# Attention scores as 64-row products in the two halves of the array, with q's norm factor moved into the exponential

## The chip, the cores and the metric

The kernel runs on one core of a Trainium2 chip. The metric is the device time of one launch in microseconds (us), median of the runs shown. A core has a matrix engine (PE, with its weight loads as PEld), a vector engine (DVE), an activation engine (ACT), a general engine (POOL) and a queue engine that issues transfers (SP). Matrix products write to PSUM, which has eight banks here, shared out by the kernel under three tags: `mm` (3), `at` (4) and `tr` (1).

## The reference

One layer of a trunk: a norm, one projection to q, k, v and three convolution inputs, sliding-window attention beside a short gated convolution, an output projection, and a squared-ReLU MLP. S is 2048, D is 1024, 8 heads of 64, 2 key/value heads (each serves 4 heads), window and block 128. What the change touches is this:

```python
q = rms_norm(q, q_norm_g[l])          # over the 64 of each head
k = rms_norm(k, k_norm_g[l])
...
sc = jnp.einsum('bnqhgd,bnkhd->bnhgqk', qb, kw).astype(jnp.float32) * scale
...
sc = jnp.where(mask[None, :, None, None], sc, NEG_INF)
...
p = jax.nn.softmax(jnp.concatenate([sc, sink], axis=-1), axis=-1)[..., :-1]
o = jnp.einsum('bnhgqk,bnkhd->bnqhgd', p.astype(v.dtype), vw)
```

## The kernel before, in words

All large products are made of three: an operand is split into a high part (rounded to fp32r) and a low part (the rest), and high x high, high x low and low x high are summed in PSUM (`mm3`, lines 276 to 280).

The 2048 rows go through the mixers in four chunks of 512 (`mixers`, line 1031), each of four blocks of 128 rows; `b` counts blocks from 0 to 15. The MLP follows: its up products are line 1454, its down products line 1571. In the mixers, two streams of work are woven together. One is attention block by block: `qk_norm` (line 675), `qk_transpose` (689), `softmax` (712), `values` (752). The other is `besides` (978), a generator of the large products: the convolution's inputs (`pc`, `px`, `pb`), the output projection (`pout`), and q, k, v of the next chunk (`pz`). The table `FILL` says how many steps of the second are taken between the pieces of the first, the table `PRIO` shifts the priority of the first, and a scheduler then sets each engine's order when the program is built. So a block's score products stand on PE either in one run, or one by one between large products.

For one block of 128 rows, before the change:

- `qk_norm` squares the 640 columns of q and k (line 679), sums by head (681), takes the power -1/2 on POOL (192, 193), multiplies all of q and k by that factor `rq` (684) and by the norm weights (687).
- `qk_transpose` turns q (four 128x128 transposes, line 697) and k (699) on PE. q's turned columns hold two heads each, one in partitions 0 to 63 and one in 64 to 127. Each head gets an operand `qt` of 128 rows, its high part in one half of the partitions and its low part in the other (702, 703). k gets, for each key/value head, two such operands `kw`, with the parts so placed that both products of a head are a full 128 rows deep (704 to 707).
- `softmax` makes two products per head, of 128 rows and 256 columns (128 keys of the block before and 128 of this one; 128 columns in block 0): 16 products a block at line 724, two heads to a bank of tag `at`. ACT copies this block's half out of the bank (732), and DVE writes the earlier block's scores over the keys that lie ahead of the query, one head at a time (735). Maximum (737, 738), eight exponentials with their sums (741), the sink (745, 746) and the division (749) follow.

The first products of a block after the scores are the transposes of its probabilities (line 760). The norm weights are loaded in `load_gains` (496, 497) and q's is scaled by 1/8 on POOL (1104). Chunk 0 has its own start (`first_chunk`, line 518), with hand-ordered engines; it writes q into `z` at line 622. Later chunks write it at line 663.

Of the kernel before, what the change touches and what calls it, by code (L numbers as in the profile page):

```python
# [16 lines left out]
P = 128  # L17
# [87 lines left out]
def hymba_layer(  # L105
# [60 lines left out]


# [320 lines left out]
    g_qk = const.tile([P, 2, DH], F32, name="g_qk")  # L488
# [5 lines left out]
    def load_gains(part):  # L494
        if not part:
            nc.sync.dma_start(g_qk[:, 0, :], q_norm_g[0].partition_broadcast(P))
            nc.sync.dma_start(g_qk[:, 1, :], k_norm_g[0].partition_broadcast(P))
            nc.sync.dma_start(sink, sinks[0].partition_broadcast(P))
            return
        for t in range(3):  # L500
            nc.sync.dma_start(cw[:, :, t], conv_w[0][t].rearrange("(i p) -> p i", p=P))
        nc.sync.dma_start(g_cols, mlp_norm_g[0].rearrange("(k p) -> p k", p=P))
        for kv in range(KVH):
            nc.sync.dma_start(
                g_y[kv * DH : (kv + 1) * DH, 0, :],
                attn_out_g[0][kv * GQ * DH : (kv + 1) * GQ * DH].rearrange("(i d) -> d i", d=DH),
            )
        nc.sync.dma_start(g_y[:, 1, :], conv_out_g[0].rearrange("(i p) -> p i", p=P))
# [9 lines left out]
    def first_chunk(first):  # L518
# [102 lines left out]
        for t in range(NT):  # L621
            nc.scalar.activation(z0[t][:, :AW], pzs[t], AF.Copy, scale=rs0[:, t : t + 1])
# [14 lines left out]
    with tc.tile_pool(name="mix_small", bufs=1) as mix_small, tc.tile_pool(name="mix", bufs=1) as mix:  # L637
# [3 lines left out]
        kw = mix.tile([P, 2, KVH, 2, P], F32R, name="kw")  # L641
# [6 lines left out]
        def project_qkv(c, h, z):  # L648
# [5 lines left out]
            for pc, t in ((0, 0), (0, 1), (1, 0), (0, 2), (0, 3), (1, 1), (1, 2), (1, 3)):  # L654
# [8 lines left out]
                nc.scalar.copy(z[t][:, pc * AW : pc * AW + n], ps)  # L663
                if pc and not t:
                    qk_norm(c * NT, z[0])
# [6 lines left out]
        nh = HEADS + KVH  # L672
        mix_small.tile([P, 8], F32, name="mix_pad")

        def qk_norm(b, zt):
# [8 lines left out]
            nc.vector.tensor_tensor(zqk, zqk, rq[:, :, None].to_broadcast([P, nh, DH]), op=ALU.mult)  # L684
            for i, (h0, h1) in enumerate(((0, HEADS), (HEADS, nh))):
                nc.vector.tensor_tensor(
                    zqk[:, h0:h1], zqk[:, h0:h1], g_qk[:, i, None, :].to_broadcast([P, h1 - h0, DH]), op=ALU.mult
                )
        def qk_transpose(b, zt):
# [3 lines left out]
            lo, hi = slice(0, DH), slice(DH, P)  # L693
            qt = mix.tile([P, HEADS // 2, 2, P], F32R, tag="qt", name=f"qt_{nm}", bufs=1)
            pt = bank("at", f"ptq_{nm}")
            for j in range(4):
                nc.tensor.transpose(pt[:, j * P : (j + 1) * P], zt[:, j * P : (j + 1) * P], ident)
            pk = bank("at", f"ptk_{nm}")[:, :P]
            nc.tensor.transpose(pk, zt[:, O_K:O_V], ident)
            p3 = pt.rearrange("p (j q) -> p j q", j=4)  # L700
            for i, (a, o) in enumerate(((lo, hi), (hi, lo))):
                nc.scalar.copy(qt[a, :, i, :], p3[a])
                nc.vector.tensor_tensor(qt[o, :, i, :], p3[a], qt[a, :, i, :].bitcast(F32), op=ALU.subtract)
                nc.scalar.copy(kw[a, i, i, own, :], pk[a])
                nc.scalar.copy(kw[o, 1 - i, i, own, :], pk[a])
                nc.vector.tensor_tensor(kw[o, i, i, own, :], pk[a], kw[a, i, i, own, :].bitcast(F32), op=ALU.subtract)
# [5 lines left out]
        def softmax(b, qt):  # L712
# [6 lines left out]
            for pr in range(HEADS // 2):  # L719
                kv = pr * 2 // GQ  # L720
                ps = bank("at", f"psc_{nm}_{pr}").rearrange("p (h s k) -> p h s k", h=2, s=2)
                for j in range(2):
                    for r in range(2):
                        nc.tensor.matmul(  # L724
                            ps[:, j].rearrange("p s k -> p (s k)")[:, :nk],
                            qt[:, pr, j, :],
                            kw[:, r, kv, :, :].rearrange("p s k -> p (s k)")[:, :nk],
                            start=r == 0,
                            stop=r == 1,
                        )  # L730
                s2 = sc[:, pr * 2 : pr * 2 + 2, :]
                nc.scalar.copy(s2, ps[:, :, own, :])  # L732
                for j in range(2):
                    other = ps[:, j, 1 - own, :] if b else neg.to_broadcast([P, P])
                    nc.vector.copy_predicated(s2[:, j, :], later, other)  # L735
            ngm = mix_small.tile([P, HEADS], F32, tag="ngm", name=f"ngm_{nm}", bufs=2)
            nc.vector.tensor_reduce(ngm, sc, axis=AX.X, op=ALU.max, negate=True)
            nc.vector.tensor_tensor(ngm, ngm, nsink, op=ALU.min)  # L738
            den = mix_small.tile([P, HEADS], F32, tag="den", name=f"den_{nm}", bufs=2)
            for hd in range(HEADS):  # L740
                nc.scalar.activation(  # L741
                    sc[:, hd, :], sc[:, hd, :], AF.Exp, bias=ngm[:, hd : hd + 1], accum_out=den[:, hd : hd + 1]
                )
# [287 lines left out]
        def mixers(c, before, h, z):  # L1031
# [20 lines left out]
            def scores(t):  # L1052
# [3 lines left out]
                with ahead(1):  # L1056
                    sc = softmax(c * NT + t, qt)
                if t + 1 < NT:
                    with ahead(2):
                        qk_norm(c * NT + t + 1, z[t + 1])  # L1060
                return sc

            if not c:
                qk_norm(0, z[0])
# [38 lines left out]
        with tc.issue_after(rs0_in):  # L1103
            nc.gpsimd.tensor_scalar(g_qk[:, 0, :], g_qk[:, 0, :], DH**-0.5, None, op0=ALU.mult)
# [506 lines left out]
```

## Time and profile before

| what | value |
|---|---|
| time, median of 3 runs | 1917.67 us (1916.55 to 1918.78) |
| profiled execution: its span, first to last instruction | 1913.4 us |
| median less that span | 4.3 us |
| PE busy | 1907.7 us, 8930 products |
| PEld busy | 1591.1 us |
| DVE busy | 1202.7 us, 1857 instructions |
| ACT busy | 829.4 us, 1557 instructions |
| POOL busy | 274.4 us, 477 instructions |
| granted PE clock | 1.000 |

No time of the profiled execution is given beside its span; the 4.3 us between the span and the median of the runs is taken as what lies around a span. A product's recorded duration is longer than the distance to the next one, since products overlap on PE; what a product costs is read from the distances between starts. In a row of the timeline the columns are start, duration of the stretch, engine, line, operation, output and inputs, rows x columns of the weights, shape of the operand, and how many were merged.

### The profile page before, as it was taken

The numbers are of one execution on the slowest core, as the hardware profiler recorded it, in microseconds if no ns is written. First come the engines' busy times: TensorE is split into PE (matmuls) and PEld (weight loads), VectorE is DVE, ScalarE is ACT, GpSimd is POOL, SyncE is SP. The second block draws the span as 40 slices with busy tenths as digits, with TensorE's granted clock in tenths as the row PEclk, the third lists the DMA queues.
The fourth block names the chain that finished last, engine by engine and source line by source line (L and its number), as shares of the span: only waits on it lengthen the run. The fifth ranks groups of instructions, "written<-read, shape, count | busy, mean of one in ns | idle before, by whom it ended". The sixth has DMA issues, their size and how long they took to land.

```text
span 1913.4 us, 24557 instructions
## 1 busy us (share of the span) xinstructions
PE 1907.7 (100%) x8930; PEld 1591.1 (83%) x8930; DVE 1202.7 (63%) x1857; ACT 829.4 (43%) x1557; POOL 274.4 (14%) x477
## 2 busy tenths in 40 slices
PE   9999999999999999999999999999999999999999
PEld 8888888888888888888888888888888888888887
DVE  5895567448467759998788766666534334457531
ACT  6564245335445346544555545453332332232320
POOL 2123212302221112233101111111000000100000
PEclk9999999999999999999999999999999999999999
DMA  9984844564578688777576544448954457766631
GB/s 305 333 320 120 329 189 177 213 227 160 203 266 277 215 294 251 221 215 244 195 233 213 175 145 159 140 148 321 364 198 150 138 171 224 281 228 213 217 124 55
DMA packets 232792, 413.80 MB, mean 216 GB/s; under 512 B 51672, under 2 KB 136416, under 8 KB 219872
## 3 DMA queue, kind: packets, MB, share of 16 engines
q1 hardware_dynamic: 203840, 336.59, 52.0%
q0 software_dynamic: 15424, 51.40, 6.9%
q10 hardware_dynamic: 13408, 24.26, 3.4%
q8 instruction: 70, 1.15, 0.2%
q14 instruction: 50, 0.41, 0.1%
HBM read 286.35 MB, written 125.83 MB: 215 GB/s over the span
## 4 chain that ended last, share of the span: by engine, by line
PE 99%; DVE 0%; POOL 0%; issue 0%; ACT 0%; DVEq 0%; POOLq 0%
PE u L1454 32%; PE d L1571 32%; PE pout L278 3%; PE pout L280 3%; PE pout L279 3%; PE pz L278 2%; PE pz L280 2%; PE pz L279 2%; PE psc_b L724 2%; PE pb_c L280 2%; PE pb_c L279 2%; PE pb_c L278 2%; PE px_c L278 2%; PE px_c L279 2%; PE px_c L280 2%; PE po_b L812 1%
## 5 line engine op out<-in xcount | busy, mean ns | idle before, releaser
L1454 PE MATMUL u<-op_x,wop 128*128 128x512 f32 x2688 | 609.7, 389 | 0.0
L1571 PE MATMUL d<-op_w,op_f 128*128 128x512 f32 x2691 | 609.5, 389 | 0.0
L1571 PEld LDWEIGHTS d<-op_w,op_f 128*128 128x128 f32 x2691 | 504.8, 188 | 104.7
L1454 PEld LDWEIGHTS u<-op_x,wop 128*128 128x128 f32 x2688 | 504.3, 188 | 105.3 <-issue 0.3
L434 DVE TENSOR_TENSOR op_f<-op_f 128x1024 fp32r<-128x1024 f32 x112 | 136.8, 1224 | 235.6 <-ACT op_f L433 235.4
L433 ACT CAST op_f<-op_f 128x1024 fp32r<-128x1024 f32 x112 | 117.7, 1051 | 349.5 <-DMA op_f<-fop 349.0
L452 ACT CAST wop<-wu 128x512 fp32r<-128x512 f32 x156 | 96.1, 619 | 92.0 <-PE u L1454 88.3
L453 DVE TENSOR_TENSOR wop<-wu,wop 128x512 fp32r<-128x512 f32 x156 | 110.2, 708 | 31.8 <-ACT wop L452 16.7
L1190 POOL DMA_DIRECT2D fop<-s x96 | 52.1, 542 | 443.2 <-DVE s L1193 436.7
L1196 DVE TENSOR_TENSOR u<-u,u 128x512 f32<-128x512 f32 x128 | 87.7, 685 | 19.4 <-PE u L1454 19.2
L434 DVE TENSOR_TENSOR op_w<-raw,op_w 128x1024 fp32r<-128x1024 f32 x56 | 68.3, 1221 | 28.8 <-ACT op_w L433 28.8
L433 ACT CAST op_w<-raw 128x1024 fp32r<-128x1024 f32 x56 | 58.8, 1052 | 48.4 <-PE d L1571 26.3
L1202 ACT ACTIVATE u<-u 128x512 f32<-128x512 f32 x64 | 40.5, 632 | 56.5 <-DVE u L1196 54.3
L741 ACT ACTIVATE sc_b<-sc_b,ngm_b 128x128 f32<-128x128 f32 x128 | 49.7, 389 | 30.0 <-DVE ngm_b L738 30.0
L773 POOL TENSOR_SCALAR_AFFINE_SELECT pp_b<-pp_b 128x512 fp32r<-128x512 f32 x60 | 41.3, 701 | 134.6 <-ACT pp_b L766 66.1
L1403 POOL DMA_DIRECT2D wds<-raw x16 | 8.5, 533 | 329.9 <-DVE raw L1401 329.9
L453 DVE TENSOR_TENSOR wop<-wu_s,wop 128x512 fp32r<-128x512 f32 x64 | 45.9, 718 | 11.9 <-ACT wop L452 11.7
L452 ACT CAST wop<-wu_s 128x512 fp32r<-128x512 f32 x64 | 39.4, 620 | 29.3 <-PE u L1454 24.9
L278 PE MATMUL pout<-w_wo,yt_c 128*128 128x512 f32 x128 | 51.5, 402 | 0.0
L280 PE MATMUL pout<-w_wo,yt_c 128*128 128x512 f32 x128 | 51.0, 398 | 0.0
L279 PE MATMUL pout<-w_wo,yt_c 128*128 128x512 f32 x128 | 50.2, 393 | 0.0
L735 DVE COPY_PREDICATED sc_b<-later,psc_b 128x128 f32<-128x128 int32 x120 | 29.4, 296 | 32.0 <-ACT sc_b L732 31.7
(265 smaller groups left out, 3119.0 us busy)
## 6 DMA issues: line engine op xcount, KB each, us to landing
op_f<-fop SPq DMA_DIRECT2D x112, 512.0 KB, 4.3
raw<-in_w_down_dram SPq DMA_DIRECT2D x72, 512.0 KB, 4.1
wu<-in_w_up_dram SPq DMA_DIRECT2D x128, 256.0 KB, 3.8
w_wo<-wo SPq DMA_DIRECT2D x24, 1024.0 KB, 6.7
fop<-s POOLq DMA_DIRECT2D x96, 256.0 KB, 2.6
fop<-u ACTq DMA_DIRECT2D x64, 256.0 KB, 2.6
op_x<-xop SPq DMA_DIRECT2D x28, 512.0 KB, 6.0
w_q<-q SPq DMA_DIRECT2D x12, 1024.0 KB, 6.7
```

The source lines that it names most:

```text
L278: nc.tensor.matmul(ps, st(0), mv(0), start=first, stop=False)
L279: nc.tensor.matmul(ps, st(0), mv(1), start=False, stop=False)
L280: last_sum[0] = nc.tensor.matmul(ps, st(1), mv(0), start=False, stop=last).ins
L433: nc.scalar.copy(op[:, 0], raw)
L434: nc.vector.tensor_tensor(op[:, 1], raw, op[:, 0].bitcast(F32), op=ALU.subtract)
L452: splits.append(nc.scalar.copy(hi, blk).ins)
L453: lows.append(nc.vector.tensor_tensor(lo, blk, hi.bitcast(F32), op=ALU.subtract).ins)
L741: nc.scalar.activation(sc[:, hd, :], sc[:, hd, :], AF.Exp, bias=ngm[:, hd : hd + 1], accum_out=den[:, hd : hd + 1])
L1190: eng.dma_start(fop_dram[tb][ORDER_DOWN.index(i)][n // 2][:, n % 2], b)
L1196: return nc.vector.tensor_tensor(dst, ps, b, op=ALU.add).ins
L1454: nc.tensor.matmul(pt, wops[i][:, a, k, :], xops[tb, p][k // 2][:, b, k % 2, :], start=p not in GOES_ON and k + j == 0, stop=k + j == NB + ...
L1571: nc.tensor.matmul(ps[tb][j][:, cs], fs[tb][:, a, k, j * P : (j + 1) * P], w[:, b, k, cs], start=first and p not in GOES_ON and k + n == 0 ...
```

## The change

- Heads are stored so that a group of 128 columns of q holds one head of each key/value head (`by_pair`, used where q is written to `z`). After the transpose, partitions 0 to 63 hold a head that uses key head 0, and 64 to 127 a head that uses key head 1.
- `qt` and `kw` hold the high and the low part of both halves in the same partitions. A score is the sum of three products of 64 rows (high x high, high x low, low x high), with the two key heads' products issued in turn, into two different banks: 24 products a block.
- q is not multiplied by its norm factor any more. The factor is applied to the negated maximum and given to the exponential as its scale, head by head. k is still multiplied by its factor.
- The two norm weights and 1/8 are multiplied into one column `g_qk`, applied to turned k as it is copied out of PSUM.
- The masked write takes two heads in one instruction.

```diff
-            nc.sync.dma_start(g_qk[:, 0, :], q_norm_g[0].partition_broadcast(P))
-            nc.sync.dma_start(g_qk[:, 1, :], k_norm_g[0].partition_broadcast(P))
+            for kv in range(KVH):
+                for i, g in enumerate((q_norm_g, k_norm_g)):
+                    nc.sync.dma_start(g_qk2[kv * DH : (kv + 1) * DH, i : i + 1], g[0].rearrange("(d i) -> d i", i=1))
...
-            nc.scalar.activation(z0[t][:, :AW], pzs[t], AF.Copy, scale=rs0[:, t : t + 1])
+            nc.scalar.activation(by_pair(z0[t]), by_kv(pzs[t]), AF.Copy, scale=rs0[:, t : t + 1])
...
-                nc.scalar.copy(z[t][:, pc * AW : pc * AW + n], ps)
+                if pc:
+                    nc.scalar.copy(z[t][:, AW:], ps)
+                else:
+                    nc.scalar.copy(by_pair(z[t]), by_kv(ps))
...
-            nc.vector.tensor_tensor(zqk, zqk, rq[:, :, None].to_broadcast([P, nh, DH]), op=ALU.mult)
-            for i, (h0, h1) in enumerate(((0, HEADS), (HEADS, nh))):
-                nc.vector.tensor_tensor(
-                    zqk[:, h0:h1], zqk[:, h0:h1], g_qk[:, i, None, :].to_broadcast([P, h1 - h0, DH]), op=ALU.mult
-                )
+            zk = zqk[:, HEADS:]
+            nc.vector.tensor_tensor(zk, zk, rq[:, HEADS:, None].to_broadcast([P, KVH, DH]), op=ALU.mult)
+            return rq
...
-            for i, (a, o) in enumerate(((lo, hi), (hi, lo))):
-                nc.scalar.copy(qt[a, :, i, :], p3[a])
-                nc.vector.tensor_tensor(qt[o, :, i, :], p3[a], qt[a, :, i, :].bitcast(F32), op=ALU.subtract)
-                nc.scalar.copy(kw[a, i, i, own, :], pk[a])
-                nc.scalar.copy(kw[o, 1 - i, i, own, :], pk[a])
-                nc.vector.tensor_tensor(kw[o, i, i, own, :], pk[a], kw[a, i, i, own, :].bitcast(F32), op=ALU.subtract)
-                nc.vector.tensor_tensor(
-                    kw[a, 1 - i, i, own, :], pk[a], kw[a, i, i, own, :].bitcast(F32), op=ALU.subtract
-                )
+            nc.scalar.copy(qt[:, 0], p3)
+            nc.vector.tensor_tensor(qt[:, 1], p3, qt[:, 0].bitcast(F32), op=ALU.subtract)
+            nc.scalar.activation(kw[:, 0, own, :], pk, AF.Copy, scale=g_qk)
+            nc.vector.scalar_tensor_tensor(
+                kw[:, 1, own, :], pk, g_qk, kw[:, 0, own, :].bitcast(F32), op0=ALU.mult, op1=ALU.subtract
+            )
...
-            for pr in range(HEADS // 2):
-                kv = pr * 2 // GQ
-                ps = bank("at", f"psc_{nm}_{pr}").rearrange("p (h s k) -> p h s k", h=2, s=2)
+            for g0 in range(0, GQ, 2):
+                pss = [bank("at", f"psc_{nm}_{g0}_{kv}").rearrange("p (h s k) -> p h s k", h=2, s=2) for kv in range(KVH)]
                 for j in range(2):
-                    for r in range(2):
-                        nc.tensor.matmul(
-                            ps[:, j].rearrange("p s k -> p (s k)")[:, :nk],
-                            qt[:, pr, j, :],
-                            kw[:, r, kv, :, :].rearrange("p s k -> p (s k)")[:, :nk],
-                            start=r == 0,
-                            stop=r == 1,
-                        )
+                    for n, (a, r) in enumerate(((0, 0), (0, 1), (1, 0))):
+                        for kv in range(KVH):
+                            rows = slice(kv * DH, (kv + 1) * DH)
+                            nc.tensor.matmul(
+                                pss[kv][:, j].rearrange("p s k -> p (s k)")[:, :nk],
+                                qt[rows, a, g0 + j, :],
+                                kw[rows, r].rearrange("p s k -> p (s k)")[:, :nk],
+                                start=n == 0,
+                                stop=n == 2,
+                            )
...
-                for j in range(2):
-                    other = ps[:, j, 1 - own, :] if b else neg.to_broadcast([P, P])
-                    nc.vector.copy_predicated(s2[:, j, :], later, other)
+                    other = ps[:, :, 1 - own, :] if b else neg[:, :, None].to_broadcast([P, 2, P])
+                    nc.vector.copy_predicated(s2, later[:, None, :].to_broadcast([P, 2, P]), other)
...
+            nc.vector.tensor_tensor(by_kv1(ngm), by_kv1(ngm), by_pair1(rq), op=ALU.mult)
...
-                    sc[:, hd, :], sc[:, hd, :], AF.Exp, bias=ngm[:, hd : hd + 1], accum_out=den[:, hd : hd + 1]
+                    sc[:, hd, :],
+                    sc[:, hd, :],
+                    AF.Exp,
+                    bias=ngm[:, hd : hd + 1],
+                    scale=rq[:, i : i + 1],
+                    accum_out=den[:, hd : hd + 1],
...
-            nc.gpsimd.tensor_scalar(g_qk[:, 0, :], g_qk[:, 0, :], DH**-0.5, None, op0=ALU.mult)
+            nc.gpsimd.tensor_tensor(g_qk, g_qk2[:, :1], g_qk2[:, 1:], op=ALU.mult)
+        with tc.issue_after(rs0_in):
+            nc.gpsimd.tensor_scalar(g_qk, g_qk, DH**-0.5, None, op0=ALU.mult)
```

Two places on PE's order show how the score products stand. The first is block 1 (in chunk 0), where they stand in one run between products of the convolution (`pb_c0`, 128x512). In the names, `psc_b1_0` is a bank of block 1's scores, `kw` and `qt_b1` its operands; 128x256 is the output. Before:

```order
L280 MATMUL pb_c0_0_1_973<-h0_a0_250,w_wb0_1_905 128x512
L724 MATMUL psc_b1_0_996<-kw_631,qt_b1_942 128x256 x4
L724 MATMUL psc_b1_1_1004<-kw_631,qt_b1_942 128x256 x4
L724 MATMUL psc_b1_2_1012<-kw_631,qt_b1_942 128x256 x4
L724 MATMUL psc_b1_3_1020<-kw_631,qt_b1_942 128x256 x4
L278 MATMUL pb_c0_0_1_973<-h0_a0_250,w_wb0_0_904 128x512
```

The same place on PE after the change, its first nine rows (`psc_b1_0_0` is the bank of key head 0 and `psc_b1_0_1` that of key head 1; 16 more rows of the same kind follow before the next product of the convolution):

```order
L296 MATMUL pb_c0_0_1_962<-h0_a0_250,w_wb0_1_902 128x512
L742 MATMUL psc_b1_0_0_985<-kw_634,qt_b1_939 128x256
L742 MATMUL psc_b1_0_1_986<-kw_634,qt_b1_939 128x256
L742 MATMUL psc_b1_0_0_985<-kw_634,qt_b1_939 128x256
L742 MATMUL psc_b1_0_1_986<-kw_634,qt_b1_939 128x256
L742 MATMUL psc_b1_0_0_985<-kw_634,qt_b1_939 128x256
L742 MATMUL psc_b1_0_1_986<-kw_634,qt_b1_939 128x256
L742 MATMUL psc_b1_0_0_985<-kw_634,qt_b1_939 128x256
L742 MATMUL psc_b1_0_1_986<-kw_634,qt_b1_939 128x256
```

Sixteen full products have become 24 half ones that alternate between the halves of the array, still in one run. The second place is block 4 (in chunk 1) on PE, where the scores stand between the convolution's products (`px_c1`). Before:

```order
L724 MATMUL psc_b4_0_2358<-kw_631,qt_b4_2289 128x256
L280 MATMUL px_c1_0_0_2469<-h0_h1_1425,w_wx01_1_2466 128x512
L724 MATMUL psc_b4_0_2358<-kw_631,qt_b4_2289 128x256
L278 MATMUL px_c1_0_0_2469<-h0_h1_1425,w_wx01_0_2465 128x512
L724 MATMUL psc_b4_0_2358<-kw_631,qt_b4_2289 128x256
L279 MATMUL px_c1_0_0_2469<-h1_h1_1426,w_wx01_0_2465 128x512
L724 MATMUL psc_b4_0_2358<-kw_631,qt_b4_2289 128x256
L280 MATMUL px_c1_0_0_2469<-h0_h1_1425,w_wx01_1_2466 128x512
```

After, in block 4, on PE:

```order
L742 MATMUL psc_b4_2_0_2350<-kw_634,qt_b4_2271 128x256
L295 MATMUL px_c1_0_1_2490<-h1_h1_1413,w_wx01_0_2442 128x512
L742 MATMUL psc_b4_2_1_2351<-kw_634,qt_b4_2271 128x256
L296 MATMUL px_c1_0_1_2490<-h0_h1_1412,w_wx01_1_2443 128x512
L742 MATMUL psc_b4_2_0_2350<-kw_634,qt_b4_2271 128x256
L294 MATMUL px_c1_0_1_2490<-h0_h1_1412,w_wx01_0_2442 128x512
L742 MATMUL psc_b4_2_1_2351<-kw_634,qt_b4_2271 128x256
L295 MATMUL px_c1_0_1_2490<-h1_h1_1413,w_wx01_0_2442 128x512
```

Here too three half products stand where two full ones stood, and a full 512-column product still stands between one half product and the next. Counted over the whole program, 256 score products in 113 runs become 384 in 157 runs; 140 of these runs are one to three products long and hold 161, and 17 runs of four to 24 hold the other 223.

More of the change, by code (lines that the diff above doesn't have):

```diff
@@ L165, in zrow, with by_kv, by_kv1, by_pair1 @@
         return pool.tile([P, O_B], F32, tag="z", name=name, bufs=NT)
+    def by_kv(b):
+        return b.rearrange("p (v g d) -> p v g d", v=KVH, g=GQ)
+    def by_kv1(r):
+        return r.rearrange("p (v g) -> p v g", v=KVH)
+    def by_pair1(r):
+        return r[:, :HEADS].rearrange("p (g v) -> p v g", v=KVH)
+    def by_pair(zt):
+        return zt[:, :AW].rearrange("p (g v d) -> p v g d", v=KVH, g=GQ)
     ident = const.tile([P, P], F32, name="ident")
@@ L672, in hymba_layer @@
         nh = HEADS + KVH
+        rqs = {}
         mix_small.tile([P, 8], F32, name="mix_pad")
```

31 lines of the change are left out of this document (17 added, 14 removed).

## The prediction

> **What bounds the kernel now.** I read the page first, for who is busy, and its chain of waits, for who sets the end:
>
> ```profile
> span 1913.4 us, 24557 instructions
> PE 1907.7 (100%) x8930; PEld 1591.1 (83%) x8930; DVE 1202.7 (63%) x1857; ACT 829.4 (43%) x1557; POOL 274.4 (14%) x477
> PE 99%; DVE 0%; POOL 0%; issue 0%; ACT 0%; DVEq 0%; POOLq 0%
> ```
>
> PE has work in all of the span, and the chain is PE itself for 99% of it. DVE and ACT are busy for 63% and 43%. The view of waits, limited to PE, has a single row:
>
> ```profile
> PE idle L579 <- POOL ident L172: 1.6, 1, 1.6
> ```
>
> That one is at the very start. So an edit changes the time by what it changes in PE's own products, and by waits that it would newly make. Next, what a product costs. The groups by line, and the timeline of PE around block 1's scores (in one run) and block 4's (one by one):
>
> ```profile
> L1454 PE MATMUL u<-op_x,wop 128*128 128x512 f32 x2688 | 609.7, 389 | 0.0
> ...
> L724 PE MATMUL psc_b<-kw,qt_b 128*128 128x256 f32 x240 | 47.1, 284 | 0.0
> ```
>
> ```profile
> 78.63 2.08 PE L724 MATMUL psc_b<-kw,qt_b 128*128 128x256 f32 x16
> ...
> 80.55 0.40 PE L278 MATMUL pb_c<-h_a,w_wb 128*128 128x512 f32 x1
> ```
>
> ```profile
> 226.13 0.28 PE L724 MATMUL psc_b<-kw,qt_b 128*128 128x256 f32 x1
> 226.25 0.40 PE L280 MATMUL px_c<-h_h,w_wx 128*128 128x512 f32 x1
> 226.48 0.28 PE L724 MATMUL psc_b<-kw,qt_b 128*128 128x256 f32 x1
> ```
>
> A 512-column product stands 609.7 / 2688 = 0.227 us after the one before, though its record lasts 0.389: the records overlap, and distances are the cost. A score product in a run costs (80.55 - 78.63) / 16 = 0.120. One that stands alone costs 226.48 - 226.13 - 0.227 = 0.123. Block 0's have 128 columns:
>
> ```profile
> 59.93 1.90 PE L724 MATMUL psc_b<-kw,qt_b 128*128 128x128 f32 x16
> 61.67 0.45 PE L278 MATMUL px_c<-h_a,w_wx 128*128 128x512 f32 x1
> ```
>
> They cost (61.67 - 59.93) / 16 = 0.109. From 512 to 256 columns the cost falls by 0.107, so half of that again would leave 0.120 - 0.053 = 0.067 for 128. It is 0.109: something that doesn't shrink with the columns takes at least that long for each product, and the weight load, one per product, is the candidate. All scores now: 16 x 0.109 + 240 x 0.121 = 30.8 us.
>
> **The change part by part.** *Score products.* 256 full products become 384 half ones, with as many columns as before. A half product has half the rows, and nothing in the three spacings above depends on rows, so alone it should cost what a full one does. The gain can only come from two halves that run together. The order after the change has 223 half products in 17 runs of four or more and 161 in 140 short runs, mostly alone between 512-column products that use all rows; those find no partner. The trace before has no product in half the rows, so what a pair costs is bounded from both sides:
>
> - Nothing runs together: each half product costs what a full one does, 24 x 0.109 + 360 x 0.120 = 45.8, so +15.0.
> - Streams overlap but loads follow one another: in runs the load sets the pace. That is 24 x 0.109 for block 0, 199 x 0.109 for the other products in runs and 161 x 0.122 for those in short runs, together 2.6 + 21.7 + 19.6 = 43.9, so +13.1.
> - A pair costs what one full product does: block 0 has 12 x 0.109, the other runs of four or more have 101 pair places (a run of odd length leaves one alone) x 0.120, the short runs 142 x 0.122; 1.3 + 12.1 + 17.3 = 30.7, so -0.1. Even in this best case the runs only give back what the lone products lose.
>
> I take the middle of the first two, +14, since both follow from the row nearest to the case (0.109 a product at half the columns), and pairing rests on nothing that this trace shows.
>
> *Change of shape.* Each of the 157 runs means two changes between full products and half ones, 314 in all. The trace has one product with few rows, `pg`, whose weights have 8:
>
> ```profile
> 2.59 1.49 PE L579 MATMUL idle<-ident 128*128 128x128 f32 x6
> 4.01 0.27 PE L583 MATMUL pg<-ident,g_rows 8*128 8x8 f32 x1
> 4.21 1.11 PE L540 MATMUL pt_a<-ident,x 128*128 128x128 f32 x4
> 5.12 1.06 PE L579 MATMUL idle<-ident 128*128 128x128 f32 x4
> ```
>
> Products here stand about 0.214 apart, so the last of the six starts at 3.66. `pg` follows 0.35 later and `pt_a` 0.20 after that: 0.55 for two distances that would be 0.43. Two changes cost at most 0.12 here, 0.06 each, and a wait for the loaded rows may be in it; the low end is nothing. The far end is that PE empties first: a 512-column record outlasts the distance by 0.389 - 0.227 = 0.162. So 314 changes cost 0 to 19 us by `pg`, and 51 by a full emptying. The forecast takes nothing, and the emptying is a rival.
>
> *DVE and ACT.* The groups that change:
>
> ```profile
> L703 DVE TENSOR_TENSOR qt_b<-ptq_b,qt_b 64x512 fp32r<-64x512 f32 x32 | 22.0, 689 | 7.8 <-ACT qt_b L702 7.1
> L684 DVE TENSOR_TENSOR z<-z,rq_b 128x640 f32<-128x640 f32 x16 | 14.5, 908 | 26.1 <-POOL rq_b L193 26.1
> L706 DVE TENSOR_TENSOR kw<-ptk_b,kw 64x128 fp32r<-64x128 f32 x32 | 9.0, 282 | 0.6 <-ACT kw L705 0.3
> L735 DVE COPY_PREDICATED sc_b<-later,psc_b 128x128 f32<-128x128 int32 x120 | 29.4, 296 | 32.0 <-ACT sc_b L732 31.7
> L738 DVE TENSOR_TENSOR ngm_b<-ngm_b,nsink 128x8 f32<-128x8 f32 x16 | 2.6, 160 | 0.2
> L702 ACT CAST qt_b<-ptq_b 64x512 fp32r<-64x512 f32 x32 | 18.6, 580 | 17.6 <-PE ptq_b L697 9.2 <-DVE qt_b L703 7.0 <-PE psc_b L724 1.1
> L705 ACT CAST kw<-ptk_b 64x128 fp32r<-64x128 f32 x32 | 8.3, 260 | 0.4
> L741 ACT ACTIVATE sc_b<-sc_b,ngm_b 128x128 f32<-128x128 f32 x128 | 49.7, 389 | 30.0 <-DVE ngm_b L738 30.0
> ```
>
> One of two 0.69 us subtractions goes, all but a fifth of line 684's 0.91 (est. 0.7), about the same again for the norm weights of line 687 over the same columns, three of four 0.28 subtractions for `kw` (0.84), and some 0.1 of each pair of masked writes (est. 0.4 a block); 0.16 comes in for the scaled maximum: 3.2 us a block, 51 for 16 blocks, off DVE. ACT loses one of two 0.58 casts and three of four 0.26 casts, 1.4 a block, 22 in all; if the scale from memory adds 0.1 to each of 128 exponentials, 13 of it come back. No row has PE waiting for either engine, so I cost all this at nothing. If that cover were gone (the fill products between scores and probabilities), a later exponential would delay line 760's transposes; with ACT and DVE both shorter there is less of that than before, and I allow 2 us either way.
>
> *Waits that move.* A pair of banks is now let go after 12 products (1.4 us at 0.120) instead of one bank after four, so ACT's first copy starts about 1 us later. Behind it in ACT's queue stand casts of weights, and products of `besides` cover both. The exponential now also waits for `rq`, but q's transposes no longer do, so that factor has more time than before. SP issues four small loads in place of two, ahead of `sink`, and POOL one product of one column more; neither has a wait of PE behind it in the view above, and both stand in the first microseconds behind x and the weights. Nothing for them.
>
> *Sum.* 1913.4 + 14 = 1927.4 of span. The median of the runs shown is 4.3 above this span, so 1931.7, say 1932.
>
> **The rivals.** *A: pairs run together, changes of shape are free.* Then -0.1 from above, within 2 or 3: about 1918. For it: the two halves' products alternate and write different banks. By the Trainium skill, TensorE: Matmul & The Clock Gate, Part 3, products in different row groups run at once (four of 32 rows gave 3.07 times the rate). No run here shows it yet, and by that rule the sum would be this rival's. Against it: 0.109 for each load, if two loads don't run together.
>
> *B: a change of shape makes PE empty.* With pairs together and 314 changes at 0.06 to 0.162, +19 to +51: 1937 to 1969, the middle 1953; without pairs up to +66, 1984. It decides from about 0.05 a change, where it outweighs what pairing could bring. The Trainium skill, TensorEngine Tiling (Array Packing), Key Properties, says that changing the tiling mode drains the engine, without a time; by that rule this rival holds, and `pg`, at 0.06 or less a change, speaks for its low end.
>
> *C: faster.* A lone half product leaves the other half free, and the next full product, or its load, gets ahead there. If a lone half cost 0.061 instead of 0.122, the 142 places would save 8.7: with pairs, 1909. It decides when the distance from one lone score product to the next falls below 0.32, from 0.35 now. Against it: full products need all rows, and block 0's 0.109 is not bound by columns.
>
> **How the numbers follow.** The forecast has 0.39, A 0.22, B 0.29, C 0.10. About 0.2%, 4 us, is what a measurement of this kernel can tell from no change. A with its 3 us is nearly all "same" (0.20, the rest slower), C is faster, and the forecast and B are slower: 0.10, 0.20 and 0.70. The range begins under A with a part of C, 1913, and ends at B's 1969; outside are most of C and B without pairs, together under 0.2. The forecast's own range is 1929 to 1936.
>
> **What would show it.** In block 1's run, the distance from the first half product to the next convolution product, over 24: 0.109 to 0.120 bears the forecast out, 0.060 means pairs (A). In chunk 1, from one lone half product to the next across a 512-column one: 0.35 is no price for shape, 0.47 or more is B, under 0.32 is C. PE's waits should stay near 1.6 us, and DVE lose some 50 us. A wait of PE for ACT or DVE in the mixers, or a gain of over 5 us, would make the working wrong.

## The result and the profile after

| what | before | after |
|---|---|---|
| median of 4 runs | 1918.22 us (1916.55 to 1920.19) | 2044.03 us (2039.95 to 2045.91) |
| ratio, 95% interval | | 1.0655 (1.064 to 1.067) |
| profiled execution: span | 1913.4 us | 2044.2 us |
| stage of the mixers (start to first up product) | 690.5 us | 804.5 us |
| stage of the up products | 609.6 us | 623.1 us |
| stage of the down products | 613.3 us | 616.6 us |

The change costs 126 us, far above the range. The prediction had the sign, and neither the size nor the parts. The page of the kernel after, first the span, the busy times, the granted clock of PE in 40 slices, and the chain of waits by engine:

```profile
span 2044.2 us, 24584 instructions
...
PE 2031.5 (99%) x9058; PEld 1623.2 (79%) x9058; DVE 1156.2 (57%) x1713; ACT 821.6 (40%) x1493; POOL 276.8 (14%) x478
...
PEclk9999878999997899999999999999999999999999
...
PE 82%; DMA 0%; issue 0%; POOL 0%; DVE 0%; ACT 0%; DVEq 0%; ACTq 0%
```

PE is still the bound and still shows 99% busy, but its record is 124 us longer for 128 more products. DVE lost 46.5 us, ACT 7.8. What is new is the clock: 7s and 8s stand in two places where before there were only 9s. Next the stages after, by windows (columns: length, then busy time and count for PE, PEld, DVE, ACT and POOL, granted clock, share of the DMA engines, GB/s):

```profile
0.00:804.50 804.50, 795.62 (x3680) 615.32 (x3681) 398.01 (x747) 315.90 (x777) 148.75 (x266) 0.93 0.57 203
804.50:1427.60 623.10, 623.10 (x2690) 503.17 (x2689) 479.73 (x696) 331.51 (x543) 105.38 (x168) 1.00 0.63 199
1427.60:2044.20 616.60, 612.77 (x2692) 504.66 (x2690) 278.46 (x270) 174.16 (x174) 22.72 (x44) 1.00 0.60 205
```

The same three before the change:

```profile
0.00:690.50 690.50, 688.64 (x3551) 582.17 (x3552) 445.41 (x891) 323.79 (x841) 147.95 (x265) 1.00 0.65 237
690.50:1300.10 609.60, 609.60 (x2690) 504.33 (x2689) 478.99 (x696) 330.89 (x543) 103.75 (x168) 1.00 0.62 203
1300.10:1913.40 613.30, 609.43 (x2692) 504.57 (x2690) 278.31 (x270) 174.75 (x174) 22.72 (x44) 1.00 0.60 206
```

114.0 us of the 130.8 lie in the mixers, where the scores are. The other 16.8 lie in the MLP, whose code the change doesn't touch and whose clock is 1.00. Groups of the kernel after that answer to the prediction's:

```profile
L1482 PE MATMUL u<-op_x,wop 128*128 128x512 f32 x2688 | 623.3, 393 | 0.0
...
L742 PEld LDWEIGHTS psc_b<-kw,qt_b 64*128 64x128 f32 x384 | 47.3, 207 | 49.7 <-issue 48.8
L742 PE MATMUL psc_b<-kw,qt_b 64*128 64x256 f32 (+1 forms) x384 | 84.8, 371 | 0.0
...
L762 ACT ACTIVATE sc_b<-sc_b,ngm_b,rq_b 128x128 f32<-128x128 f32 x128 | 61.5, 482 | 27.5 <-DVE ngm_b L758 27.5
```

An up product now stands 623.3 / 2688 = 0.232 us from the next, 0.227 before. The weight loads of the scores have a wait of 48.8 us ahead of them that the trace can lay on nothing but the issue. The scale from memory costs an exponential 482 - 389 = 93 ns. Now the two places that the prediction named, on PE's timeline. Block 1's run:

```profile
81.14 0.39 PE L296 MATMUL pb_c<-h_a,w_wb 128*128 128x512 f32 x1
81.45 1.69 PE L742 MATMUL psc_b<-kw,qt_b 64*128 64x256 f32 x24
83.07 0.50 PE L294 MATMUL pb_c<-h_a,w_wb 128*128 128x512 f32 x1
83.41 0.40 PE L295 MATMUL pb_c<-h_a,w_wb 128*128 128x512 f32 x1
```

The 24 half products take 83.07 - 81.45 = 1.62, or 0.068 each. Twelve pairs at 0.12 make 1.44, so halves do run together, and 0.18 is left over at the run's end. The distance into the run is 0.31 where two such products stand 0.227 apart, and the product behind it stands 0.34 ahead of its follower. The three excesses, 0.08, 0.18 and 0.11, make 0.37 for the run. Chunk 1, lone halves, first at full clock and then a little later:

```profile
232.79 0.38 PE L742 MATMUL psc_b<-kw,qt_b 64*128 64x256 f32 x1
233.10 0.49 PE L296 MATMUL px_c<-h_h,w_wx 128*128 128x512 f32 x1
233.53 0.38 PE L742 MATMUL psc_b<-kw,qt_b 64*128 64x256 f32 x1
...
239.73 0.58 PE L742 MATMUL psc_b<-kw,qt_b 64*128 64x256 f32 x1
...
240.96 0.58 PE L742 MATMUL psc_b<-kw,qt_b 64*128 64x256 f32 x1
```

From one lone half to the next it is 0.74 (0.35 before), later 1.23. In between, the granted clock has fallen, which a window shows:

```profile
237.10:261.00 23.90, 23.90 (x47) 12.76 (x47) 6.21 (x11) 2.13 (x6) 0.19 (x1) 0.50 0.33 136
```

Nine such stretches at 0.50 lie in the mixers, 112.6 us together (the clock record of the trace: 3.4, 23.9, 20.5, 10.2 and 6.8 us in chunks 0 and 1, 3.4, 20.5, 17.1 and 6.8 in chunk 3). Before there was none. In the 3.4 us ahead of eight of the nine, PE's record has no gap and holds four to eight score products among larger ones; ahead of the first, at 63.1 us, PE has waited 1.5 us for ACT. Last, PE's waits, the first three of eight rows that make 8.7 us:

```profile
PE pt_a L322 <- DVE h_h L327: 2.4, 4, 0.8
PE idle L597 <- POOL ident L188: 1.6, 1, 1.6
PE ptq_b L717 <- ACT sc_b L752: 1.5, 1, 1.5
```

All but the second are new, 7.1 us in sum. The prediction had no wait of PE for DVE or ACT.

**The theory** after this reading: each run of half products costs about 0.39 us beside the work in it, whatever its length (0.74 - 0.35); lone halves between full products also bring PE's clock down; buffers that have moved cost the MLP its 17 us; and the order that the other edits bring costs a few us of waits. **The rivals:** the loss is one of 24 products instead of 16; the other edits make it; the price is one per half product; the clock falls by half products as such.

### The profile page after: what moved, and what is told of

Same layout as the page of the kernel before. It is cut to its first block, busy times and chain, and to the rows that moved or that the text cites. A ratio compares the mean times of both kernels' runs of the same rounds, so it can differ in the third digit from the quotient of the medians.

```text
span 2044.2 us, 24584 instructions
## 1 busy us (share of the span) xinstructions
PE 2031.5 (99%) x9058; PEld 1623.2 (79%) x9058; DVE 1156.2 (57%) x1713; ACT 821.6 (40%) x1493; POOL 276.8 (14%) x478
## 4 chain that ended last, share of the span: by engine, by line
PE 82%; DMA 0%; issue 0%; POOL 0%; DVE 0%; ACT 0%; DVEq 0%; ACTq 0%
PE u L1482 30%; PE d L1599 30%; PE pout L294 2%; PE pout L296 2%; PE pout L295 2%; PE psc_b L742 2%; PE pz L294 1%; PE pz L295 1%; PE pz L296 1%; PE po_b L838 1%; PE pc_c L294 1%; PE pb_c L296 1%; PE pc_c L295 1%; PE pb_c L295 1%; PE pc_c L296 1%; PE pb_c L294 1%
## 5 line engine op out<-in xcount | busy, mean ns | idle before, releaser
L1482 PE MATMUL u<-op_x,wop 128*128 128x512 f32 x2688 | 623.3, 393 | 0.0
L742 PEld LDWEIGHTS psc_b<-kw,qt_b 64*128 64x128 f32 x384 | 47.3, 207 | 49.7 <-issue 48.8
L742 PE MATMUL psc_b<-kw,qt_b 64*128 64x256 f32 (+1 forms) x384 | 84.8, 371 | 0.0
L449 ACT CAST op_w<-raw 128x1024 fp32r<-128x1024 f32 x56 | 58.6, 1048 | 45.1 <-PE d L1599 20.5
L762 ACT ACTIVATE sc_b<-sc_b,ngm_b,rq_b 128x128 f32<-128x128 f32 x128 | 61.5, 482 | 27.5 <-DVE ngm_b L758 27.5
L752 ACT COPY sc_b<-psc_b 128x256 f32<-128x256 f32 x64 | 21.8, 374 | 119.8 <-PE psc_b L742 119.7
L754 DVE COPY_PREDICATED sc_b<-later,psc_b 128x256 f32<-128x256 int32 x60 | 24.4, 440 | 66.2 <-ACT sc_b L752 66.1
L294 PE MATMUL pout<-w_wo,yt_c 128*128 128x512 f32 x128 | 52.0, 406 | 0.3 <-DVE x L989 0.3
```

Source lines behind the costliest of these rows:

```text
L294: nc.tensor.matmul(ps, st(0), mv(0), start=first, stop=False)
L449: nc.scalar.copy(op[:, 0], raw)
L742: nc.tensor.matmul(pss[kv][:, j].rearrange("p s k -> p (s k)")[:, :nk], qt[rows, a, g0 + j, :], kw[rows, r].rearrange("p s k -> p (s k)")[ ...
L762: nc.scalar.activation(sc[:, hd, :], sc[:, hd, :], AF.Exp, bias=ngm[:, hd : hd + 1], scale=rq[:, i : i + 1], accum_out=den[:, hd : hd + 1],)
L1482: nc.tensor.matmul(pt, wops[i][:, a, k, :], xops[tb, p][k // 2][:, b, k % 2, :], start=p not in GOES_ON and k + j == 0, stop=k + j == NB + ...
```

## The experiments

**e_pad** puts the buffers back, as was meant, with an unused tile in the pool of constants (`g_qk` has become 448 bytes smaller in each partition, so that all that is allotted behind it has moved):

```diff
+    const.tile([P, 125], F32, name="g_pad")
```

> The changed kernel with 500 bytes per partition put back into the constants, so that every later buffer lies where it lay before the change. In the changed kernel's trace the MLP's up stage lasts 623.3 us for 2688 products (0.232 each) at the full clock, before the change 609.7 (0.227), though nothing in it was edited. Theory: buffers moved to other addresses make these products slower; then the up stage comes back to 610 and the time falls by 13 to 14, to about 2030, while the mixers stay as they are. Rival: the up stage is slower for something that comes out of the mixers (clock, transfers, order); then it stays at 623 and the time at 2044.

Measured 2041.34 us, ratio 1.0652 (1.0607 to 1.0696); up stage 623.2. A miss, but of the edit: 500 bytes become 512 as tiles are aligned, so the buffers came to lie 64 bytes behind their old places instead of 448 ahead of them. The up stage is as slow at both, and these two differ by 512. The right pad is 112 columns, and **e_pad448** has it:

```diff
+    const.tile([P, 112], F32, name="g_pad")
```

> The changed kernel with 448 bytes put back. The first try put back 500, which takes 512 since buffers begin at multiples of 32 bytes; with the 64 that the two new columns take, every later buffer then lay 64 bytes past its old place, as in the changed kernel (448 before it, the same rest by 512). Now they lie where they lay. Theory: the up stage comes back from 623 to 610 us, the down stage from 616.5 to 613.4, and the mixers lose some 5, so about 21 less than the changed kernel: 2022, give or take the 10 by which the clock moved the last run. Rival (the address isn't it): 623 and 2041.

2022.21 us, 1.0556 (1.053 to 1.0581); up stage 610.4, down 613.3, mixers 794.7. So 22 us come back. Of the 25.8 between the two profiled spans (2018.4 here), 16.0 are in the MLP, as the theory has it, and 9.8 in the mixers, which hold 88.7 us at half clock here and not 112.6. That time differs from one execution to the next (the four runs of this kernel go from 2016.06 to 2031.16), so the 9.8 are not shown to come from the buffers. Its counterpart, **e_shift64**, moves the buffers of the kernel before by 64 bytes and does nothing else:

```diff
+    const.tile([P, 16], F32, name="g_pad")
```

> The kernel before with one unused constant of 64 bytes, nothing else, and the same order on every engine. Theory: up stage 623, down stage 616.5, mixers some 5 longer: 1916 + 21 = 1937. Rival (the address isn't it): 1916.

1933.53 us, 1.0093 (1.0079 to 1.0106). The up products of this kernel, and their stage by windows:

```profile
L1455 PE MATMUL u<-op_x,wop 128*128 128x512 f32 x2688 | 623.3, 393 | 0.0
```

```profile
690.60:1313.70 623.10, 623.10 (x2689) 503.22 (x2689) 480.33 (x696) 331.21 (x543) 103.18 (x168) 1.00 0.63 198
```

The same 623.3 and 623.1 as in the kernel after, from 64 unused bytes, and nothing in the mixers, which end at 690.6 (690.5 before); the 5 us expected there did not come. This part of the loss is the place of the buffers. Which operand minds it, `op_x` or `wop`, wasn't separated.

**e_rest** is the kernel before with all edits but the half products: factor in the exponential, both norm weights on k, masks by two heads, scores as 16 full products.

```diff
-            nc.vector.tensor_tensor(zqk, zqk, rq[:, :, None].to_broadcast([P, nh, DH]), op=ALU.mult)
...
+            zk = zqk[:, HEADS:]
+            nc.vector.tensor_tensor(zk, zk, rq[:, HEADS:, None].to_broadcast([P, KVH, DH]), op=ALU.mult)
+            nc.vector.tensor_tensor(zk, zk, g_qk[:, 0, None, :].to_broadcast([P, KVH, DH]), op=ALU.mult)
...
+            nc.vector.tensor_tensor(ngm, ngm, rq[:, :HEADS], op=ALU.mult)
...
+                    scale=rq[:, hd : hd + 1],
```

> The kernel before with the other edits alone: q's factor as the exponential's scale, both norm weights on k (here ahead of the turn, not on turned k), masks by two heads; scores stay 16 full products. Theory: all of it is hidden behind PE: 1916 to 1920, DVE some 40 us less busy. Rival (the exponential with a scale from memory, 0.48 in place of 0.39, or the later wait for the factor holds up PE): over 1925.

1922.99 us, 1.0036 (1.0022 to 1.0051), mixers 698.3. The edits that shorten DVE make the kernel slower, by 7 us, where 4 at most were expected. PE's waits in it, two of five rows:

```profile
PE pt_m L374 <- DVE xt_m L375: 2.7, 1, 2.7
...
PE pt_a L306 <- DVE h_h L311: 1.5, 2, 1.1
```

New waits are 5.2 us in sum, and the clock is at half for 3.4 us behind the first. Each is one place where the scheduler, given other lengths, has put DVE's work later than PE wants it. That these places come from the order is read from the trace, not tried.

**e_half** is the other part alone: the kernel before with the 24 half products and the order of heads that they need, everything else as it was.

```diff
+            qt = mix.tile([P, 2, GQ, P], F32R, tag="qt", name=f"qt_{nm}", bufs=1)
...
+                    for n, (a, r) in enumerate(((0, 0), (0, 1), (1, 0))):
+                        for kv in range(KVH):
+                            rows = slice(kv * DH, (kv + 1) * DH)
+                            nc.tensor.matmul(
+                                pss[kv][:, j].rearrange("p s k -> p (s k)")[:, :nk],
+                                qt[rows, a, g0 + j, :],
+                                kw[rows, r].rearrange("p s k -> p (s k)")[:, :nk],
```

> Kernel before with the half products alone: the order of heads in q, the halves of q and of k, 24 products of 64 rows; q is still multiplied by its factor and its weights, k by its own before the turn, masks by one head, and the buffers lie where they did. Price by change and clock: the kernel after with its buffers put back took 2022, the other edits took 7 of that, so about 2015 (2007 to 2023), mixers near 788, mean clock about 0.978. Rival, the loss lies in the other edits or in the order that they bring (masks, weights on k, the scale in the exponential): well under 1990.

2020.51 us, 1.0549 (1.0532 to 1.0567); mixers 793.8, up 611.7. Its granted clock in 40 slices:

```profile
PEclk9999889999998999999999999999999999999999
```

So half products alone make nearly the whole loss of the mixers, and the clock falls with them. Of the 78.4 us at half clock here, 10.2 follow waits of PE (1.9 us for `h_h`, 3.4 us for `o_b`); ahead of the rest PE's record has no gap, as in the kernel after. The rival that lays it on the other edits is out.

**e_full24** and **e_full24p** keep the order of the kernel after, its 24 products a block and its 157 runs, and let each product use all 128 rows, so that each score also holds the other key head's share; the first has the pad of 125 columns, the second that of 112.

```diff
-                            rows = slice(kv * DH, (kv + 1) * DH)
+                            rows = slice(0, P)
```

> The changed kernel with the bytes put back and each of the 24 score products of a block made over all 128 rows, in the same order and at the same 157 places, so each score wrongly holds the other key head's share too. Theory (the price is the change between full and half products, and the clock that falls with it): 128 products more at 0.12 than before the change, no change of shape, clock 1.00: 1933. Rival 1 (what costs is products standing alone, or the other edits, or the order): it stays near 2030. Rival 2 (the forecast's own sum was right and something else added up): also 1933, but then runs of half products elsewhere must cost as much as full ones.

> The kernel with 24 full-row products a block (the same 157 places, each score also holding the other key head's share), with buffers at their old places. Theory: 1916 + 128 x 0.12 = 1931, plus up to 3 of waits: 1931 to 1934, clock 1.00. Rival (more than the count and the address separates it from the kernel before): it stays near 1950.

1952.49 us, 1.0191 (1.0176 to 1.0207), with an up stage of 623.1; and with the buffers in place (1931 to 1934 expected) 1935.05 us, 1.01 (1.0086 to 1.0113), mixers 710.5, clock 1.00 throughout. The same place in chunk 1:

```profile
231.62 0.28 PE L743 MATMUL psc_b<-kw,qt_b 128*128 128x256 f32 x1
231.73 0.40 PE L296 MATMUL px_c<-h_h,w_wx 128*128 128x512 f32 x1
231.96 0.28 PE L743 MATMUL psc_b<-kw,qt_b 128*128 128x256 f32 x1
```

From one score product to the next 0.34, against 0.74 with half the rows. 128 more products at 0.12 are 15.4 of the 20 us that its mixers gain, and 4.3 are waits. So the number of products is worth 15, and the change of rows in the same order another 84 in the mixers (794.7 - 710.5).

**e_low600** and **e_lowd300** gather the half products: higher priority for a block's score products, and the high parts last, so that they start when everything is there. The first has the pad of 125 columns and raises all blocks; the second has the pad of 112 and raises only the blocks of chunks 1 and 3.

```diff
+                with tc.high_priority(offset=300) if b // NT % 2 else nullcontext():
...
-                    for n, (a, r) in enumerate(((0, 0), (0, 1), (1, 0))):
+                        for n, (a, r) in enumerate(((0, 1), (1, 0), (0, 0))):
```

> The changed kernel with the bytes put back, the score products given priority 600 and the products that need the low parts issued first, so that the order holds 17 runs of 24 half products (34 changes of shape in place of 314). Theory: a run of 24 with the products beside it takes 0.1 us less than before the change (2.27 against 2.37 from the last full product ahead to the second behind it), so 1915 to 1920 and a clock of 1.00. Rival (half products are slow by themselves, or the clock falls because half the array idles): over 1930, with a clock below 1.00.

> The changed kernel with buffers at their old places, the products that need the low parts first, and priority 300 for the scores of chunks 1 and 3 alone, so that the order holds 19 runs (38 changes of shape in place of 314). Theory (price is the change of shape, and the run with priority 600 lost 14 us to waits that the priority made): the mixers take 690 to 698, clock 1.00, 1915 to 1924, where the upper end has the 7 us of waits that the other edits alone showed. Rival (half products cost by themselves): over 1930.

1953.41 us, 1.0189 (1.0174 to 1.0205) with 17 runs and the moved buffers; 1930.45 us, 1.0073 (1.006 to 1.0087) with 19 runs and the old places. Both miss what was expected (1915 to 1920 and 1915 to 1924), and both lie over the 1930 that the rival, half products slow by themselves, had set. In the first, the MLP is 16.7 us longer than before, as with other moved buffers, and PE's new waits are 14.2 us, 7.0 of them of the scores for `kw`; its 10.2 us at half clock stand behind waits for `kw` of 4.3 and 2.2 us. The second is 92 us under e_pad448, with the same products in another order and the clock at 1.00 throughout. Its waits, the first two of twelve rows that make 12.5 us:

```profile
PE ptq_b L718 <- DVE sc_b L756: 2.2, 2, 1.4
PE pt_a L322 <- DVE h_h L327: 2.0, 4, 0.8
```

By the sum, its mixers should be 19 x 0.39 = 7.4 for the runs, 192 pairs in place of 256 products (12 x 0.109 + 180 x 0.120 - 30.8 = -7.9) and 10.9 of new waits: +10.4. Measured +13.4; 3 us are not placed. So what lies over the expectation is mostly waits, and these 3 us at most are left for half products that are slow by themselves. No version that was found beats the kernel before.

**e_bench** measures the price by itself. X is a full product of 512 columns, H one of 64 rows and 256 columns.

```diff
+    for _ in range(16):
+        X(4)
+        H(0)
...
+    for _ in range(40):
+        X()
+        H(0)
+        H(1)
```

> A kernel that leaves out the layer: TensorE alone runs fixed patterns of 512-column full-row products (X) and 256-column products in one half of the array's rows (H), and then writes what stood in PSUM; its whole time is not compared with anything. Price by change (the theory): each run of half products between X products costs about 0.37 us beside the work, however many it holds. Then X + a full-row 256-column product repeats in about 0.347 us; 4 X + one H in 4 x 0.227 + 0.12 + 0.37 = 1.40, 4 X + a pair (both halves) also in 1.40, 4 X + two pairs in 1.52, 4 X + four H of the same half in 1.76 (products of one half do not run side by side), 4 X + one H of 512 columns in about 1.50, 2 X + one H in 0.87, X + one H and X + a pair in 0.64 at full clock; the run of 120 H of alternating halves takes about 0.06 us each. Clock (the theory): it falls to about half within X + H and X + pair, where TensorE streams some half of the time, and stays at 1.00 in 4 X + H and 4 X + pair. Rival, a price per half product: 4 X + pair 1.8, 4 X + two pairs 2.5. Rival, the clock has to do with half products as such: it then also falls in the run of 120 or in 4 X + H.

The launch took 440.29 us. The stretches of the patterns by windows, in this order: X + full product of 256 columns (40 times), 4 X + H (16), 4 X + pair (16), 4 X + four H of one half (16), 4 X + two pairs (16), 120 H in turn, 4 X + H of 512 columns (16), 2 X + H (24), X + pair (40), and X + H (40) in two pieces:

```profile
31.30:45.64 14.34, 14.34 (x82) 12.24 (x81) 0.00 (x0) 0.00 (x0) 0.00 (x0) 1.00 0.00 0
59.37:82.39 23.02, 23.02 (x82) 13.67 (x81) 0.00 (x0) 0.00 (x0) 0.00 (x0) 1.00 0.00 0
96.14:119.27 23.13, 23.13 (x98) 13.76 (x97) 0.00 (x0) 0.00 (x0) 0.00 (x0) 1.00 0.00 1
133.00:161.50 28.50, 28.50 (x129) 19.25 (x129) 0.00 (x0) 0.00 (x0) 0.00 (x0) 1.00 0.00 1
175.22:200.15 24.93, 24.93 (x129) 15.53 (x128) 0.00 (x0) 0.00 (x0) 0.00 (x0) 1.00 0.00 1
213.96:221.34 7.38, 7.38 (x122) 7.25 (x121) 0.00 (x0) 0.00 (x0) 0.00 (x0) 1.00 0.01 2
235.07:259.82 24.75, 24.75 (x81) 13.67 (x80) 0.00 (x0) 0.00 (x0) 0.00 (x0) 1.00 0.00 1
273.57:296.93 23.36, 23.36 (x74) 11.59 (x73) 0.00 (x0) 0.00 (x0) 0.00 (x0) 1.00 0.00 1
310.66:340.41 29.75, 29.75 (x122) 14.89 (x121) 0.00 (x0) 0.00 (x0) 0.00 (x0) 1.00 0.00 1
354.14:362.50 8.36, 8.36 (x24) 4.23 (x23) 0.00 (x0) 0.00 (x0) 0.00 (x0) 1.00 0.00 0
362.50:397.84 35.34, 35.34 (x59) 16.30 (x58) 0.00 (x0) 0.00 (x0) 0.00 (x0) 0.50 0.00 0
```

Between the stretches stand 60 X each time; from 45.64 to 59.37 that is 0.229 an X. X and the full product of 256 columns repeat in 0.35 (below), so that product is 0.12. With these two the work of a cycle is known, and the rest is the price:

| pattern | a cycle | work in it | price |
|---|---|---|---|
| 4 X + H | 1.44 | 0.916 + 0.12 | 0.40 |
| 4 X + pair | 1.45 | 0.916 + 0.12 | 0.41 |
| 4 X + two pairs | 1.56 | 0.916 + 0.24 | 0.40 |
| 4 X + four H of one half | 1.78 | 0.916 + 0.48 | 0.38 |
| 4 X + H of 512 columns | 1.55 | 0.916 + 0.229 | 0.40 |
| 2 X + H | 0.97 | 0.458 + 0.12 | 0.39 |
| X + pair | 0.74 | 0.229 + 0.12 | 0.39 |

One price of 0.38 to 0.41 us for each run of half products, whatever the run holds: two changes, about 0.2 each on average. A price per half product would have given 4 X + two pairs 2.5. Halves of one side do not run together, halves of both sides do: the 120 take 7.38 / 120 = 0.0615 each. X + H and X + pair were expected at 0.64 and take 0.74; that was my slip, 0.29 of price in place of the same 0.37. Where the price sits shows with the loads beside the products. First the loads and products of one cycle of 4 X + H, then X with a full product of 256 columns:

```profile
62.23 0.76 PEld L37 LDWEIGHTS x_lone<-mv,st 128*128 128x128 f32 x4
62.23 1.20 PE L37 MATMUL x_lone<-mv,st 128*128 128x512 f32 x4
63.36 0.18 PEld L48 LDWEIGHTS lone<-mv,st 64*128 64x128 f32 x1 [0.37 <-issue]
63.36 0.38 PE L48 MATMUL lone<-mv,st 64*128 64x256 f32 x1
```

```profile
39.88 0.40 PE L37 MATMUL x_full<-mv,st 128*128 128x512 f32 x1
39.88 0.19 PEld L42 LDWEIGHTS full<-mv,st 128*128 128x128 f32 x1
40.12 0.28 PE L42 MATMUL full<-mv,st 128*128 128x256 f32 x1
40.12 0.19 PEld L37 LDWEIGHTS x_full<-mv,st 128*128 128x128 f32 x1
40.23 0.40 PE L37 MATMUL x_full<-mv,st 128*128 128x512 f32 x1
```

Among full products a load starts with the product before its own (39.88 for the product at 40.12). At a change of shape it starts only with its own product (63.36 and 63.36), after 0.37 in which PEld has stood idle: nothing is loaded ahead across the change.

The clock: X + H ran at 1.00 for 8 us and then at 0.50 to its end, X + pair at 1.00 for all of its 30 us, though both repeat in 0.74. X + pair had been expected to fall too. So it isn't half products as such, nor the idle time of the cycle alone; what differs is that H alone leaves half the rows idle while it streams, and that its cycle holds one product less. Which of the two counts was not separated, each pattern ran once, and X + H ran last. The other patterns, with more X for each change, kept 1.00.

## Why the prediction was wrong

The sum of the measured parts, against the 130.8 us between the two profiled spans:

| part | forecast | measured | worked out |
|---|---|---|---|
| products of the scores | +14 | about 0 | pairs at 0.12, as rival A has it |
| changes of shape | 0 | +61 | 157 runs x 0.39 |
| clock | not considered | +45 | 112.6 us at half clock x (1 - 0.74 / 1.23) |
| waits of PE | 0 within 2 | +7 | 8.7 - 1.6 |
| place of the buffers | not considered | +17 | 13.5 in the up stage, 3.3 in the down stage |
| sum | +14 | +130 | |

The same sum gives e_half's mixers 61 + 78.4 x 0.4 + 10 = 102 (measured 103) and e_pad448's 61 + 88.7 x 0.4 + 7 = 103 (measured 104). The shares of price and clock rest on the distances 0.35, 0.74 and 1.23, and no run took away one and kept the other in the kernel itself. A second working bears the clock's share out: if every distance between starts in the nine stretches is set to the median at full clock of the same three products in a row, they lose 46 us.

*Score products.* The step that failed is "I take the middle of the first two, +14, since both follow from the row nearest to the case". That row, 0.109 for a full product of 128 columns, bounds loads that follow one another in all rows; loads into different halves run together, as the run at 0.068 a product and the 120 at 0.0615 show. What the forecast described is e_full24p: 1935.05, three above the 1932. The Trainium skill, TensorE: Matmul & The Clock Gate, Part 3, has tiles in different rows start about 4 ns apart, and the trace agrees: in the 120 products the second of a pair starts 3 to 4 ns behind the first.

*Change of shape.* The step that cost most is "The forecast takes nothing, and the emptying is a rival". Rival B was the mechanism, and its condition decided: the cycle of a lone half is 0.74, where 0.47 was the sign for B. Its price was too low at both ends, 0.06 to 0.162 a change against 0.2. The far end counted an emptying and not that the next load waits for it as well; the low end counted two distances around `pg`, where the price lies on three (0.08, 0.18 and 0.11 in block 1). Nor did it see at which clock `pg` stands: products of 128 columns are 0.214 apart there and 0.109 in block 0's run, and the trace has no record of the clock before 6.5 us, where full clock begins. So 0.06 a change was in all likelihood read at half clock. The Trainium skill, TensorEngine Tiling (Array Packing), Key Properties, says that a change of mode drains the engine; by that rule this rival holds, and the late loads agree with it.

*The clock.* No step of the prediction looked at what a thinner stream does to the granted clock, and the page of before, at 9 in all slices, gave no sign. The Trainium skill, TensorE: Matmul & The Clock Gate, Part 1, has a clock of full or half, set by PE's activity in windows of 3.4 us. The levels agree (1.00 and 0.50), and the stretches are multiples of 3.4 us (3.4, 6.8, 10.2, 17.1, 20.5, 23.9). It tells of idle gaps as the cause. Falls behind waits are here too (e_rest, e_half, e_low600), but the fall in X + H has none (8.36 us busy of 8.36), nor have eight of the nine in the kernel after, and there the measurement differs. A record without gaps doesn't make PE fully used: by the distances 0.35 us of each 0.74 is work, in X + pair as in X + H.

*DVE and ACT.* Sizes were right: DVE lost 46.5 us where 51 were forecast, ACT 7.8 where 22 - 13 = 9 were, the 13 for 0.1 us more in each exponential (0.093 measured). "I cost all this at nothing" was 7 us off, since new lengths brought a new order and with it waits (e_rest).

*Place of the buffers.* The edit makes a constant 448 bytes smaller. The prediction counted what the instructions do and not where the operands would then lie.

## What to carry to other kernels

By the prices measured here, half-row products save time only in long runs with a partner in the other half: a run costs 0.39 us, which is what three full products of 256 columns cost, and the 16 products of a block shrink by 4 x 0.12 = 0.48, so that even one run a block gains 0.1 us. Block 1 shows it (2.27 us from the last full product ahead of the scores to the second behind them, 2.37 before); no whole kernel here gained. Count the changes of shape in the order on PE before anything else, and where half products stand alone between full ones, look at the granted clock too. When a change alters the size of any resident tile, compare a stage that it doesn't touch: if that moves, pad the tile back first.

## What the runs showed of the hardware that was not expected

- Weight loads don't run ahead across a change between 128 and 64 rows: 0.38 to 0.41 us for a run of half products, whatever the run holds.
- PE's clock fell to 0.50 in a stream without a gap: X + H at 0.74 us a cycle fell after 8 us, X + pair at the same 0.74 did not (one execution). In the kernel the half clock cost about 45 us.
- Waits of PE of 1.5 to 4.3 us also stand ahead of 3.4 to 6.8 us at half clock (kernel after, e_rest, e_half, e_low600), though not every wait of 1.5 us does (e_full24p kept 1.00).
- Buffers 64 bytes further on made each up product 0.232 us in place of 0.227: 13.5 us in the up stage, 1.0093 (1.0079 to 1.0106) for the kernel.
